# Sum t4 of the weight blocks moved from VectorE to an accumulating DMA, and gate chunk 3 put on seven block products

## The chip, the cores and the metric

The kernel runs on one core of a Trainium2 chip. The metric is the device time of one execution in microseconds; lower is better. The kernel before takes 1500.86 us, the median of three runs (1500.27 to 1501.66).

## The reference, cut to what matters

One decoder block on a 256 x 2048 input, all in float32. Nearly all the work is in products of a 256-row activation with weight matrices:

```python
h = rms_norm(x, norm_mix_pre)
p, q, k, v, g_lr, r, gate_logits = split_combined(h @ w_in)
y_a = pool_mixer(p, w_pool, pool_scale) @ w_branch_a
o = gla_chunked(q, k, v, log_sigmoid(g_lr @ w_gate_up + b_gate) / 16)
y_b = (rms_norm(o, gla_norm) * silu(r)) @ w_branch_b
gates = sigmoid(gate_logits + b_branch_gates)
mixed = (gates[0] * y_a + gates[1] * y_b) @ w_out
x = x + rms_norm(mixed, norm_mix_post)
h = rms_norm(x, norm_ffn_pre)
f = (silu(h @ w_ffn_gate) * (h @ w_ffn_up)) @ w_ffn_down
return x + rms_norm(f, norm_ffn_post)
```

## The kernel before, in words

**Chunks.** Every weight matrix is taken in chunks of 512 columns, and each chunk is one Job. plan() (L55) lists them in order: chunks of w_in (p, r, q, k), w_branch_a, w_in again (v, and eight "gates" chunks), w_branch_b (b), w_out (out), then for three parts of the feed-forward layer the pairs gate/up and four "down" chunks. The rows of weights run over tiles of 128 (kt is their number, 16 for most chunks, 12 for "down" in the third part). The last value that plan() yields says whether a chunk is "fast".

**Float32 in three products.** A weight w is split into wh, its rounding to the format that TensorE multiplies, and wl, the rest. ScalarE makes wh (an ACTIVATE with a copy) and VectorE makes wl (a subtraction). The activation is split in the same way, and each product is wh by high, wl by high, wh by low.

**Plain chunks.** A Step (L296) takes two weight tiles of 128 x 512: SP loads them into a "raw" buffer (L307, three buffers), L316 makes wh, L320 makes wl, and 12 matmuls of 512 columns follow (L347 to L349).

**Fast chunks.** The first eight weight tiles of a fast chunk are handled as a product of two-by-two blocks, by seven block products in place of eight. The blocks of weights are b11, b12 (the first block tile) and b21, b22 (the second). SP loads each block tile with two DMAs of 512 KB (L978) into one of three buffers. The products are Parts (L353), called q1, r5, q6, q7, q2, q4 and r3. Each has 12 matmuls of 256 columns (L407 to L409), wh from L383 and wl from L387. The weights of the Parts are:

- q1: b11 as loaded; q2: b21 as loaded; r3: b22 as loaded
- r5: b12 + b11, made in the place of b12 by an accumulating DMA that GpSimd issues (L379)
- q6: t2, the former plus b22, again in the place of b12 (L368, VectorE)
- q7: t2 - b11, in the place of b11 (L370, VectorE)
- q4: t4 = b21 + t2, in the place of b21 (L372, VectorE)

The remaining eight weight tiles (four in the third part of "down") are Steps, called m0 to m3 here.

**Order.** Job.merged (L281) sets the order of the units. q1, r5, q6 and q7 of a fast chunk stand between the last units of the chunk before. Where two fast chunks follow each other, the order of the units is q2, m0, q4, q1', r3, r5', m1, q6', m2, q7', m3, and then q2', m0', q4' and so on; a dash marks the following chunk, and this document calls such a place a join. prepare_to (L981) makes wh and wl up to four units ahead of TensorE (BUFS), makes the sums of a Part two units ahead, and starts the DMA for r5 up to seven units ahead (SUMS_AHEAD). blocks() (L967) loads the block tiles when a buffer comes free: the buffer of a first block tile is given on after q4, that of a second one after r3. A scheduler puts the instructions of each engine into their final order.

**Small work.** When a chunk ends, its done function takes the results out of PSUM; for "gates" (L763) that is L768, a sigmoid, and L772. Other small work stands in the queue bg and is taken one piece per unit: after gates chunk 1 these are the six pieces of combine (L221), which make the sums of the activation's blocks for the "b" chunks with L230, L241, L235 and L236.

Of the kernel before, what the change touches and what calls it, by code (L numbers as in the profile page):

```python
# [12 lines left out]
ALU = mybir.AluOpType  # L13
# [13 lines left out]
CW = 512  # L27
# [18 lines left out]
OFF_P, OFF_Q, OFF_K, OFF_V, OFF_G, OFF_R, OFF_GA = 0, 1024, 2048, 3072, 5120, 5136, 7184  # L46
# [8 lines left out]
def plan():  # L55

    kt = D // P
    for kind, off, n in [("p", OFF_P, 2), ("r", OFF_R, 4), ("q", OFF_Q, 2), ("k", OFF_K, 2)]:
        for i in range(n):
            low = kind == "r" and i == 0  # L60
            yield kind, i, "w_in", 0, kt, OFF_G if low else off + i * CW, CW + RANK if low else CW, False
    for n in range(4):
        yield "a", n, "w_branch_a", 0, kt // 2, n * CW, CW, False
    for n in range(4):
        yield "v", n, "w_in", 0, kt, OFF_V + n * CW, CW, False
    for n in range(8):
        yield "gates", n, "w_in", 0, kt, OFF_GA + n * CW, CW, n in (2, 4, 5, 6, 7)
    for n in range(4):
        yield "b", n, "w_branch_b", 0, kt, n * CW, CW, n in (1, 3)
    for n in range(4):  # L70
        yield "out", n, "w_out", 0, kt, n * CW, CW, n < 3
    chunks = DFF // CW
    for part in range(3):
        ms = range(part * 4, min(part * 4 + 4, chunks))
        for m in ms:
            yield "gate", m, "w_ffn_gate", 0, kt, m * CW, CW, m > 0
            yield "up", m, "w_ffn_up", 0, kt, m * CW, CW, m > 0
        for n in range(4):
            yield "down", (part, n), "w_ffn_down", part * 16, 4 * len(ms), n * CW, CW, (part, n) != (2, 3)


def packed(name, w):

    import numpy as np

    out = []
    for _, _, which, k0, kt, c0, width, fast in plan():
        if which != name:
            continue
        rows = w[0, k0 * P:(k0 + kt) * P, c0:c0 + width].reshape(kt, P, width)  # L90
        if fast:
            for b in range(2):
                blocks = rows[b * 4:b * 4 + 4].reshape(4, P, 2, HW)
                out.append(blocks.transpose(2, 1, 0, 3).ravel())
            rows = rows[4 * FAST:]
        out.append(rows.reshape(-1, GK, P, width).transpose(0, 2, 1, 3).ravel())
    return np.concatenate(out)
# [3 lines left out]
def tile_hybrid_block(ctx: ExitStack, tc: tile.TileContext, *aps):  # L101
# [4 lines left out]
    act, dve, pool, pe, sync = nc.scalar, nc.vector, nc.gpsimd, nc.tensor, nc.sync  # L106
# [14 lines left out]
    def nm(s):  # L121
        uid[0] += 1
        return f"{s}_{uid[0]}"
# [10 lines left out]
    def f32(ap):  # L134
        return ap.bitcast(F32)
# [68 lines left out]
    class Act:  # L204


        def __init__(self, name, groups, tag):
            self.name = name
            self.hi = [one.tile([P, 4, T], F32R, tag=f"{tag}{g}h", name=f"{name}{g}h") for g in range(groups)]
            self.lo = [one.tile([P, 4, T], F32R, tag=f"{tag}{g}l", name=f"{name}{g}l") for g in range(groups)]  # L210
# [48 lines left out]
    class Job:  # L259
# [4 lines left out]
        def __init__(self, w, at, kt, width, fast, lhs, done, across=False, head=0, tail=0):  # L264
            self.w, self.at, self.lhs, self.kt, self.width, self.done = w, at, lhs, kt, width, done
            self.across, self.groups, self.ps, self.extra, self.fast = across, kt // GK, None, None, fast
            both = tuple(range(NT))
            self.blocks = []
            self.early = [Part(self, n) for n in EARLY] if fast else []
            w = [Step(self, g) for g in range(FAST * 4 // GK if fast else 0, self.groups)]  # L270
            m = [(w[g], (t,)) for t in both for g in range(head)]
            m += [(x, both) for x in w[head:len(w) - tail]]
            m += [(x, (t,)) for t in both for x in w[len(w) - tail:]]
            self.units = m
            if fast:
                q2, q4, r3 = [(Part(self, n), both) for n in ("q2", "q4", "r3")]
                self.units = [q2, m[0], q4, r3] + m[1:] if len(m) > 2 else [q2, q4, r3] + m
            for w, ts in self.units:
                w.uses += 1
# [16 lines left out]
    class Step:  # L296
# [13 lines left out]
        def sum(self):  # L310
            pass
# [6 lines left out]
        def low(self):  # L318
            self.lo = wp.tile([P, GK, self.j.width], F32R, tag="wl", name=nm("wl"))
            dve.tensor_tensor(self.lo, self.raw, f32(self.hi), op=ALU.subtract)  # L320
# [32 lines left out]
    class Part:  # L353
# [8 lines left out]
        def sum(self):  # L362
            b11, b12 = self.block((0, 0)), self.block((0, 1))
            b21, b22 = (self.block((1, 0)), self.block((1, 1))) if len(self.j.blocks) > 1 else (None, None)
            if self.part == "r5":
                self.start_sum()
            elif self.part == "q6":
                dve.tensor_tensor(b12, b12, b22, op=ALU.add)  # L368
            elif self.part == "q7":
                dve.tensor_tensor(b11, b12, b11, op=ALU.subtract)  # L370
            elif self.part == "q4":
                dve.tensor_tensor(b21, b21, b12, op=ALU.add)  # L372
            self.src = {"q1": b11, "r5": b12, "q6": b12, "q7": b11, "q2": b21, "q4": b21, "r3": b22}[self.part]

        def start_sum(self):

            if not self.begun and self.j.blocks:
                self.begun = True
                pool.dma_start(self.block((0, 1)), self.block((0, 0)), accum_op=ALU.add)  # L379

        def high(self):
            self.hi = wp.tile([P, 4, HW], F32R, tag="wh", name=nm("wh"))
# [2 lines left out]
        def low(self):  # L385
            self.lo = wp.tile([P, 4, HW], F32R, tag="wl", name=nm("wl"))
            dve.tensor_tensor(self.lo, self.src, f32(self.hi), op=ALU.subtract)  # L387

        def left(self, i):
            lhs, p = self.j.lhs(), self.part  # L390
            if p in COMBOS:
                while p not in getattr(lhs, "x", {}):
                    (bg.popleft() if bg else soon.pop(0)[1])()
                return tuple(a[:, i] for a in lhs.x[p])
            return lhs.get(i if p == "q1" else 4 + i, 1 if p == "q4" else 0)
# [549 lines left out]
    for kind, n, name, k0, kt, c0, width, fast in plan():  # L945
        jobs.append(Job(source[name], at[name], kt, width, fast, **kinds[kind](n)))
        at[name] += kt * P * width
# [19 lines left out]
    def blocks():  # L967

        while held and held[0] < counts_["low"]:
            held.popleft()  # L970
        while pending and pending[0][0] <= counts_["low"] + AHEAD and len(held) < BLOCKS:
            _, until, j, rows_ = pending.popleft()
            tile_ = blk.tile([P, 2, 4, HW], F32, tag="blocks", name=nm("blocks"))
            j.blocks.append(tile_)
            n = 4 * P * HW
            for i in range(2):
                at = j.at + (rows_ * 2 + i) * n
                sync.dma_start(tile_[:, i], j.w[at:at + n].rearrange("(p k c) -> p k c", p=P, k=4))  # L978
            held.append(until)

    def prepare_to(n):  # L981
        while counts_["low"] < min(n, len(order)):
            at = counts_["low"]
            blocks()
            for w in order[at:at + SUMS_AHEAD]:
                if w.part == "r5":
                    w.start_sum()
            while counts_["sum"] < min(at + 2, len(order)):
                w = order[counts_["sum"]]
                w.sum()  # L990
                counts_["sum"] += 1
            order[at].high()
            order[at].low()
            counts_["low"] += 1
        blocks()

    for c in range(1, 4):
        prepare_to(c)
        load_x(c)
# [12 lines left out]
    for n, (j, w, ts) in enumerate(units):  # L1012
        prepare_to(released + BUFS)
        if n < 7:
            transpose_in(xa, hT, n + 1, "pre")
        due = [x for x in soon if x[0] <= 0]
        soon = [[n_ - 1, f] for n_, f in soon if n_ > 0]
        for _, f in due:
            f()
        w.multiply(ts)  # L1020
        left[w] -= 1
        while released < len(order) and not left[order[released]]:
            released += 1
        ended = tuple(t for t in ts if w.part not in EARLY and last[j if w.j is j else w.j, t] == n)
        if ended:
            w.j.done(w.j, ended)
        elif bg:
            bg.popleft()()
# [50 lines left out]
```

## Time and profile before

| | us |
|---|---|
| median of three runs (1500.27 to 1501.66) | 1500.86 |
| the profiled execution | 1499.66 |
| its span, first to last instruction | 1497.9 |
| its busy TensorE / VectorE / ScalarE / GpSimd | 1481.0 / 1185.1 / 887.3 / 64.8 |
| the 41 sums of t4 on VectorE (L372) | 50.2 |
| the 41 issues of the accumulating DMA on GpSimd (L379) | 35.4 |

PE is the matmul row of TensorE, DVE is VectorE, ACT is ScalarE, POOL is GpSimd, SPq and POOLq are the queues of SyncE and GpSimd that issue DMAs. In the rows of a timeline the first two numbers are the start and the busy time, in microseconds from the start of the span; what ended an idle time before an instruction is given in brackets. Matmuls overlap, so the time of a unit is read from start to start and not from the sum of its rows.

### The profile page before, as it was taken

The page shows a single profiled execution, that of the slowest core. Times are in us where ns is not written, and L with a number is a line of the kernel's source. Part 1 is how long each engine was busy: PE and PEld are TensorE (multiplying, and loading weights), DVE is VectorE, ACT ScalarE, POOL GpSimd, SP SyncE. Part 2 cuts the span into 40 slices and gives each one's busy share as a digit, 9 for nine tenths or more (in the row PEclk, how much of TensorE's full clock was granted, in tenths as well). Part 3 has the DMA queues.
Part 4 walks back from the last instruction along what each step waited for, and adds up shares of the span by engine and source line. Part 5 has one row for each costly group of instructions (what it writes and reads, how often), then busy time and mean ns, then how long its engine had stood idle before and what let it go on. Part 6 is the DMA issues. An engine that isn't in the chain of part 4 may idle for free.

```text
span 1497.9 us, 23015 instructions
## 1 busy us (share of the span) xinstructions
PE 1481.0 (99%) x8976; PEld 1306.7 (87%) x8976; DVE 1185.1 (79%) x1319; ACT 887.3 (59%) x1150; POOL 64.8 (4%) x91
## 2 busy tenths in 40 slices
PE   9999999999999999999999999999999999999997
PEld 8988999888888888889878989998989888988886
DVE  5755445885578897799768899887889898889996
ACT  6366433555455665556656666666666665666663
POOL 2000000000000000000000000000000000000001
PEclk9999999999999999999999999999999999999999
DMA  9746655345555688558855677767776776677654
GB/s 303 265 160 196 186 186 179 127 128 166 158 174 187 196 250 259 198 169 274 261 184 155 213 223 222 226 215 225 236 217 212 229 225 218 224 232 228 201 176 141
DMA packets 85869, 307.84 MB, mean 206 GB/s; under 512 B 9804, under 2 KB 10016, under 8 KB 85504
## 3 DMA queue, kind: packets, MB, share of 16 engines
q1 hardware_dynamic: 77616, 279.15, 55.6%
q0 software_dynamic: 7440, 25.97, 9.0%
q8 instruction: 70, 1.15, 0.3%
q10 hardware_dynamic: 704, 1.25, 0.3%
q14 instruction: 39, 0.32, 0.1%
HBM read 282.74 MB, written 2.10 MB: 190 GB/s over the span
## 4 chain that ended last, share of the span: by engine, by line
PE 90%; DVE 4%; issue 3%; DMA 2%; ACT 1%; POOL 0%; SPq 0%; DVEq 0%; POOLq 0%; ACTq 0%
PE acc L347 17%; PE acc L349 17%; PE acc L348 17%; PE ac L408 5%; PE ac L407 5%; PE ac L409 5%; PE acc L409 4%; PE acc L407 4%; PE acc L408 4%; PE acc L338 3%; PE acc L336 3%; PE acc L337 3%; PE tr L662 1%; DMA raw<-in_w_in_dram 1%; PE tr L179 1%
## 5 line engine op out<-in xcount | busy, mean ns | idle before, releaser
L316 ACT ACTIVATE wh<-raw 128x1024 fp32r<-128x1024 f32 (+1 forms) x356 | 376.7, 1059 | 360.3 <-PE acc L349 186.3
L320 DVE TENSOR_TENSOR wl<-raw,wh 128x1024 fp32r<-128x1024 f32 (+1 forms) x356 | 435.1, 1224 | 183.1 <-ACT wh L316 181.5
L387 DVE TENSOR_TENSOR wl<-blocks,wh 128x1024 fp32r<-128x1024 f32 x287 | 348.9, 1222 | 73.9 <-ACT wh L383 70.4
L383 ACT ACTIVATE wh<-blocks 128x1024 fp32r<-128x1024 f32 x287 | 301.7, 1058 | 143.3 <-PE acc L349 57.1
L409 PE MATMUL ac<-wh,x 128*128 128x256 f32 x336 | 94.1, 280 | 0.0
L408 PE MATMUL ac<-wl,x 128*128 128x256 f32 x336 | 94.1, 280 | 0.0
L407 PE MATMUL ac<-wh,x 128*128 128x256 f32 x336 | 94.0, 280 | 0.0
L379 POOL DMA_DIRECT2D blocks<-blocks x41 | 35.4, 864 | 811.8 <-DVE wl L320 329.7
L347 PE MATMUL acc<-wh,h22h 128*128 128x512 f32 x176 | 70.3, 399 | 0.2 <-ACT wh L316 0.2
L348 PE MATMUL acc<-wl,h22h 128*128 128x512 f32 x176 | 69.4, 394 | 0.0
L349 PE MATMUL acc<-wh,h23l 128*128 128x512 f32 x176 | 69.4, 394 | 0.0
L347 PE MATMUL acc<-wh,h23h 128*128 128x512 f32 x176 | 69.3, 395 | 0.1
L349 PE MATMUL acc<-wh,h22l 128*128 128x512 f32 x176 | 69.2, 394 | 0.0
L348 PE MATMUL acc<-wl,h23h 128*128 128x512 f32 x176 | 69.1, 393 | 0.0
L407 PEld LDWEIGHTS ac<-wh,x 128*128 128x128 f32 x336 | 63.1, 188 | 2.6
L408 PEld LDWEIGHTS ac<-wl,x 128*128 128x128 f32 x336 | 63.0, 188 | 2.5
L409 PEld LDWEIGHTS ac<-wh,x 128*128 128x128 f32 x336 | 63.6, 189 | 0.0
L372 DVE TENSOR_TENSOR blocks<-blocks,blocks 128x1024 f32<-128x1024 f32 x41 | 50.2, 1224 | 1.1
L368 DVE TENSOR_TENSOR blocks<-blocks,blocks 128x1024 f32<-128x1024 f32 x41 | 50.1, 1222 | 0.9
L347 PE MATMUL acc<-wh,h2h 128*128 128x512 f32 (+1 forms) x128 | 50.3, 393 | 0.0
L370 DVE TENSOR_TENSOR blocks<-blocks 128x1024 f32<-128x1024 f32 x41 | 50.0, 1219 | 0.1
L348 PE MATMUL acc<-wl,h3h 128*128 128x512 f32 (+1 forms) x128 | 49.8, 389 | 0.0
(540 smaller groups left out, 4126.1 us busy)
## 6 DMA issues: line engine op xcount, KB each, us to landing
raw<-in_w_in_dram SPq DMA_DIRECT2D x148, 512.0 KB, 3.6
raw<-in_w_ffn_gate_dram SPq DMA_DIRECT2D x48, 512.0 KB, 4.4
raw<-in_w_ffn_up_dram SPq DMA_DIRECT2D x48, 512.0 KB, 4.7
blocks<-in_w_ffn_down_dram SPq DMA_DIRECT2D x44, 512.0 KB, 4.3
raw<-in_w_ffn_down_dram SPq DMA_DIRECT2D x44, 512.0 KB, 4.4
blocks<-blocks POOLq DMA_DIRECT2D x41, 512.0 KB, 6.0
blocks<-in_w_ffn_gate_dram SPq DMA_DIRECT2D x40, 512.0 KB, 4.3
blocks<-in_w_ffn_up_dram SPq DMA_DIRECT2D x40, 512.0 KB, 4.4
```

Of the source, the lines that this page charges most:

```text
L316: act.activation(self.hi, self.raw, AF.Copy)
L320: dve.tensor_tensor(self.lo, self.raw, f32(self.hi), op=ALU.subtract)
L347: pe.matmul(ps, ah, hi[:, i, cs], start=first, stop=False, skip_group_check=j.fast)
L348: pe.matmul(ps, ah, lo[:, i, cs], start=False, stop=False, skip_group_check=j.fast)
L349: pe.matmul(ps, al, hi[:, i, cs], start=False, stop=last, skip_group_check=j.fast)
L368: dve.tensor_tensor(b12, b12, b22, op=ALU.add)
L372: dve.tensor_tensor(b21, b21, b12, op=ALU.add)
L383: act.activation(self.hi, self.src, AF.Copy)
L387: dve.tensor_tensor(self.lo, self.src, f32(self.hi), op=ALU.subtract)
L407: pe.matmul(dst, ah, wh, start=i == 0 and p in ("q1", "r5"), stop=False, skip_group_check=True)
L408: pe.matmul(dst, ah, wl, start=False, stop=False, skip_group_check=True)
L409: pe.matmul(dst, al, wh, start=False, stop=i == 3 and p in EARLY, skip_group_check=True)
```

## The change

Two things change. First, chunk 3 of the gates is fast too. Second, t4 is no longer a sum on VectorE in the place of b21. An accumulating DMA, issued by GpSimd, adds b21 onto t2, in the place of b12. It may start when t2 has been used twice: by the split for q6 (its wl is the last reader) and by the sum for q7; t2_used counts that. q4 then splits b12.

```diff
-        yield "gates", n, "w_in", 0, kt, OFF_GA + n * CW, CW, n in (2, 4, 5, 6, 7)
+        yield "gates", n, "w_in", 0, kt, OFF_GA + n * CW, CW, n > 1
...
-            self.blocks = []
+            self.blocks, self.t2_used = [], 0
...
             elif self.part == "q7":
                 dve.tensor_tensor(b11, b12, b11, op=ALU.subtract)
+                self.j.t2_used += 1
             elif self.part == "q4":
-                dve.tensor_tensor(b21, b21, b12, op=ALU.add)
-            self.src = {"q1": b11, "r5": b12, "q6": b12, "q7": b11, "q2": b21, "q4": b21, "r3": b22}[self.part]
+                self.start_sum()
+                assert self.begun
+            self.src = {"q1": b11, "r5": b12, "q6": b12, "q7": b11, "q2": b21, "q4": b12, "r3": b22}[self.part]
 
         def start_sum(self):
 
-            if not self.begun and self.j.blocks:
+            j = self.j
+            if not self.begun and (j.t2_used == 2 if self.part == "q4" else j.blocks):
                 self.begun = True
-                pool.dma_start(self.block((0, 1)), self.block((0, 0)), accum_op=ALU.add)
+                pool.dma_start(self.block((0, 1)), self.block((1, 0) if self.part == "q4" else (0, 0)), accum_op=ALU.add)
...
             dve.tensor_tensor(self.lo, self.src, f32(self.hi), op=ALU.subtract)
+            self.j.t2_used += self.part == "q6"
...
-                if w.part == "r5":
+                if w.part in ("r5", "q4"):
                     w.start_sum()
```

Lines L353 to L400 of the kernel before stand three lines lower in the changed one (L387 becomes L390, L379 becomes L382), later ones four (L768 becomes L772, L978 becomes L982).

**The queue of SP at a join of the feed-forward layer, before.** blocks_10058 is the second block tile of the following chunk, blocks_9887 and blocks_10097 are first block tiles, and the raw buffers are m0, m1, m2 and m3 of one chunk:

```order
L978 DMA blocks_9887<-in_w_ffn_gate_dram 128x1024 x2
L307 DMA raw_10032<-in_w_ffn_up_dram 128x1024
L307 DMA raw_10129<-in_w_ffn_up_dram 128x1024
L307 DMA raw_10169<-in_w_ffn_up_dram 128x1024
L978 DMA blocks_10058<-in_w_ffn_gate_dram 128x1024 x2
L307 DMA raw_10204<-in_w_ffn_up_dram 128x1024
L978 DMA blocks_10097<-in_w_ffn_up_dram 128x1024 x2
```

The same place in the changed kernel, where blocks_10118 is the second block tile of the following chunk:

```order
L982 DMA blocks_9947<-in_w_ffn_gate_dram 128x1024 x2
L307 DMA raw_10092<-in_w_ffn_up_dram 128x1024
L307 DMA raw_10189<-in_w_ffn_up_dram 128x1024
L307 DMA raw_10229<-in_w_ffn_up_dram 128x1024
L307 DMA raw_10265<-in_w_ffn_up_dram 128x1024
L982 DMA blocks_10118<-in_w_ffn_gate_dram 128x1024 x2
L982 DMA blocks_10157<-in_w_ffn_up_dram 128x1024 x2
```

The load of the second block tile has moved behind the raw buffer of m3. It goes into the buffer of an older first block tile, whose last reader was the sum L372 before and is the wl of q4 now.

**VectorE at the start of gates chunk 3, before** (a plain chunk there). The first two rows are the first piece of combine, L241, L236 and L230 are further pieces, and each L320 is the wl of a Step:

```order
L230 TENSOR_TENSOR scr_4382<-o0h,o0l 128x512
L230 TENSOR_TENSOR scr_4384<-o1h,o1l 128x512
L320 TENSOR_TENSOR wl_4390<-raw_4386,wh_4388 128x1024
L241 TENSOR_TENSOR scr_4384<-scr_4382,scr_4384 128x512
L320 TENSOR_TENSOR wl_4411<-raw_4407,wh_4409 128x1024
L236 TENSOR_TENSOR ox_4363<-scr_4384,ox_4362 128x512
L230 TENSOR_TENSOR scr_4425<-o0h,o0l 128x512
L320 TENSOR_TENSOR wl_4432<-raw_4428,wh_4430 128x1024
```

The same place in the changed kernel, now a join of gates chunks 2 and 3. The two L390 are the wl of r3 and of r5', L368 is the sum for q6', and the L320 is the wl of m1:

```order
L230 TENSOR_TENSOR scr_4383<-o0h,o0l 128x512
L230 TENSOR_TENSOR scr_4385<-o1h,o1l 128x512
L390 TENSOR_TENSOR wl_4389<-blocks_3902,wh_4387 128x1024
L241 TENSOR_TENSOR scr_4385<-scr_4383,scr_4385 128x512
L390 TENSOR_TENSOR wl_4411<-blocks_4091,wh_4409 128x1024
L236 TENSOR_TENSOR ox_4363<-scr_4385,ox_4363 128x512
L230 TENSOR_TENSOR scr_4425<-o0h,o0l 128x512
L368 TENSOR_TENSOR blocks_4091<-blocks_4091,blocks_4336 128x1024
L241 TENSOR_TENSOR scr_4383<-scr_4425,scr_4383 128x512
L320 TENSOR_TENSOR wl_4433<-raw_4429,wh_4431 128x1024
```

The sum for q6' has come in ahead of the wl of m1, among the pieces of combine. The rows that follow, as far as the wl of m2:

```order
L236 TENSOR_TENSOR ox_4366<-scr_4383,ox_4365 128x512
L241 TENSOR_TENSOR scr_4425<-scr_4385,scr_4425 128x512
L390 TENSOR_TENSOR wl_4457<-blocks_4091,wh_4455 128x1024
L236 TENSOR_TENSOR ox_4361<-scr_4425,ox_4361 128x512
L230 TENSOR_TENSOR scr_4473<-o1h,o1l 128x512
L370 TENSOR_TENSOR blocks_4091<-blocks_4091 128x1024
L320 TENSOR_TENSOR wl_4480<-raw_4476,wh_4478 128x1024
```

Here the wl of q6' and the sum for q7' (L370) stand ahead of the wl of m2, and four more pieces of combine.

## The prediction

> **What bounds the kernel now.** First the page: busy time by engine.
>
> ```profile
> span 1497.9 us, 23015 instructions
> PE 1481.0 (99%) x8976; PEld 1306.7 (87%) x8976; DVE 1185.1 (79%) x1319; ACT 887.3 (59%) x1150; POOL 64.8 (4%) x91
> ```
>
> TensorE is busy for all but 17 us of the span. A share hides stages, so the next view is busy time by stretch: from left PE, PEld, DVE, ACT, POOL, then clock, DMA share and GB/s. The stretches are the gates and b chunks, the feed-forward layer from its first fast chunk on, and its third part.
>
> ```profile
> 430.00:600.00 170.00, 170.00 (x941) 146.50 (x940) 143.21 (x154) 102.08 (x126) 8.89 (x13) 1.00 0.70 218
> 820.00:1405.00 585.00, 585.00 (x3696) 525.30 (x3695) 516.40 (x517) 377.86 (x469) 23.13 (x27) 1.00 0.71 221
> 1405.00:1470.00 65.00, 63.41 (x412) 56.73 (x411) 63.73 (x69) 43.24 (x61) 2.83 (x4) 1.00 0.59 186
> ```
>
> In the first two TensorE never waits, though VectorE is busy for 84% and 88%. Only in the third is VectorE as full as TensorE (63.73 and 63.41 of 65 us), and only there does TensorE wait for wh or wl. Its two longest waits from 1400 to 1475 us (in all, times, longest):
>
> ```profile
> PE acc L347 <- ACT wh L316: 0.6, 1, 0.6
> PE ac L407 <- ACT wh L383: 0.5, 1, 0.5
> ```
>
> So time taken off VectorE is worth something in the last 65 us, 1.6 us at most (65.00 - 63.41). Elsewhere the bound is the number of matmuls.
>
> **Chunk 3 in seven products: the matmuls.** What a unit takes is read from TensorE's timeline, start to start, at one join. The units are m3, q2', m0', q4', q1'', r3', r5'', m1':
>
> ```profile
> 1060.99 0.40 PE L347 MATMUL acc<-wh,h23h 128*128 128x512 f32 x1
> ...
> 1063.76 0.28 PE L407 MATMUL acc<-wh,h21h 128*128 128x256 f32 x1
> ...
> 1065.12 0.40 PE L347 MATMUL acc<-wh,h22h 128*128 128x512 f32 x1
> ...
> 1067.89 0.28 PE L407 MATMUL acc<-wh,h21h 128*128 128x256 f32 x1
> ...
> 1069.25 0.28 PE L407 MATMUL ac<-wh,h20h 128*128 128x256 f32 x1
> ...
> 1070.67 0.28 PE L407 MATMUL acc<-wh,x 128*128 128x256 f32 x1
> ...
> 1072.05 0.28 PE L407 MATMUL ac<-wh,x 128*128 128x256 f32 x1
> ...
> 1073.46 0.39 PE L347 MATMUL acc<-wh,h22h 128*128 128x512 f32 x1
> ```
>
> A Step takes 2.77 us. q2 and q4 take 1.36 each, r3 1.38, q1 1.42, r5 1.41; q6 and q7, which write the same place as q1, I take at 1.41. Seven Parts make 9.75 us in place of four Steps, 11.08. **Term: -1.3 us.**
>
> **Chunk 3: what VectorE has to do there.** The Steps needed four wl; the Parts need seven, two sums and two subtractions of results, and they come just where the pieces of combine run. The rows of VectorE at that place before:
>
> ```profile
> 477.14 0.69 DVE L230 TENSOR_TENSOR scr<-o0h,o0l 128x512 f32<-128x512 f32 x1
> 477.74 0.69 DVE L230 TENSOR_TENSOR scr<-o1h,o1l 128x512 f32<-128x512 f32 x1
> 478.34 1.22 DVE L320 TENSOR_TENSOR wl<-raw,wh 128x1024 fp32r<-128x1024 f32 x1
> 479.48 0.68 DVE L241 TENSOR_TENSOR scr<-scr,scr 128x512 f32<-128x512 f32 x1
> 480.08 1.22 DVE L320 TENSOR_TENSOR wl<-raw,wh 128x1024 fp32r<-128x1024 f32 x1
> ```
>
> Back to back, a large operation advances VectorE by 1.14 us and a piece by 0.60. Up to 478.34 the work ahead is the same in both kernels, but for one t4 sum that ran earlier and had idle time behind it. TensorE stood here:
>
> ```profile
> 477.42 0.28 PE L407 MATMUL acc<-wh,h1h 128*128 128x256 f32 x1
> ...
> 478.83 0.28 PE L407 MATMUL acc<-wh,x 128*128 128x256 f32 x1
> ```
>
> q4 ended at 478.83. In the changed kernel q1', r3 and r5' follow (1.42 + 1.38 + 1.41), and m1 begins at 483.04. VectorE, from 478.34 by the changed order: wl of r3 (1.14), L241 (0.60), wl of r5' (1.14), L236 and L230 (1.20), the sum for q6' (1.14), L241 (0.60), so the wl of m1 starts at 484.16 and is there at 485.38, 2.1 us after its first use (483.27). Then two pieces, the wl of q6', two pieces and the sum for q7': the wl of m2 starts at 484.16 + 1.14 + 1.20 + 1.14 + 1.20 + 1.14 = 489.98 and is there at 491.20. Without waits m2 would need it at 483.04 + 2.77 + 1.41 + 0.23 = 487.45. TensorE is then 3.7 us late in all; it can take a few products with wh ahead, some 0.3 us. After that the lag ends: two pieces and two large operations lie between this and the wl of m3, 3.5 us for 4.2 us of TensorE. **Term: +3.4 us**, between 0 (if the pieces give way) and 5 (if ScalarE's roundings in between hold VectorE up).
>
> **t4 leaves VectorE.** The group of the sums on the page:
>
> ```profile
> L372 DVE TENSOR_TENSOR blocks<-blocks,blocks 128x1024 f32<-128x1024 f32 x41 | 50.2, 1224 | 1.1
> ```
>
> 50.2 us go, 1.22 a chunk. Since TensorE waited nowhere between 820 and 1405, this is worth 0 there.
>
> **t4 as a DMA: is it in time?** The trace has its like, the accumulating DMA for r5. Its rows are: issue over the whole run, time to landing from 820 to 1405, the share of the GpSimd queue in that stretch.
>
> ```profile
> L379 POOL DMA_DIRECT2D blocks<-blocks x41: 848/852/941, 31.9 to 1436.5; - x41
> ```
>
> ```profile
> DMA to landing us min/median/max: 5.0/6.0/8.0
> ```
>
> ```profile
> q0 software_dynamic: 3888, 14.16, 13.3%
> ```
>
> 27 issues (POOL, x27 above) in 13.3% of 585 us make 2.9 us of all 16 engines for one. The place is the join above. VectorE's rows are the wl of q6, the sum for t4, the wl of q4, the next sum for q6, and the wl of m1; then ScalarE's wh for q4, GpSimd's issue for r5, and SP's loads of the next second and first block tile:
>
> ```profile
> 1053.01 1.22 DVE L387 TENSOR_TENSOR wl<-blocks,wh 128x1024 fp32r<-128x1024 f32 x1
> ...
> 1059.64 1.23 DVE L372 TENSOR_TENSOR blocks<-blocks,blocks 128x1024 f32<-128x1024 f32 x1
> ...
> 1062.83 1.23 DVE L387 TENSOR_TENSOR wl<-blocks,wh 128x1024 fp32r<-128x1024 f32 x1 [0.38 <-ACT wh L383]
> ...
> 1070.44 1.23 DVE L368 TENSOR_TENSOR blocks<-blocks,blocks 128x1024 f32<-128x1024 f32 x1
> 1071.58 1.22 DVE L320 TENSOR_TENSOR wl<-raw,wh 128x1024 fp32r<-128x1024 f32 x1
> ```
>
> ```profile
> 1061.73 1.06 ACT L383 ACTIVATE wh<-blocks 128x1024 fp32r<-128x1024 f32 x1
> ```
>
> ```profile
> 1052.60 0.86 POOL L379 DMA_DIRECT2D blocks<-blocks  x1 [20.29 <-DVE wl L320]
> ```
>
> ```profile
> 1060.90 0.93 SPq L978 DMA_DIRECT2D blocks<-in_w_ffn_gate_dram  x2
> ...
> 1068.02 0.81 SPq L978 DMA_DIRECT2D blocks<-in_w_ffn_up_dram  x2
> ```
>
> t4 may start when the wl of q6 is done, at 1054.23. Alone it lands 6.0 us later, 1060.3; behind the DMA for r5 (1052.60 + 6.0 + 2.9) at 1061.5. ScalarE takes q4 at 1061.73. It is just in time by the medians and up to 1.8 us late by the longest landing (8.0). By itself that costs nothing: q4 starts on TensorE at 1067.89 and its wl is done at 1064.06. On GpSimd the next r5, due 20 us later, queues behind the wait.
>
> The Trainium skill (DMA: Bandwidth & Descriptors, "Anatomy of one DMA — SWDGE (gpsimd) path") fits such a DMA as 2.0 us plus bytes over 436 GB/s. For 512 KB that is an estimate of 3.2 us, and t4 would land at 1057.4 with 4 us to spare. The trace has 5.0 at least and does not agree; I go by the trace.
>
> **The load behind it.** The next second block tile goes into the buffer that q4 now reads last. Its load could start at 1060.90, after the sum; now it waits for the wl of q4, 1064.06. Behind it on SP stand the next first block tile, which waited until 1068.02 anyway, and the raw buffer of m0'; m3 has been moved ahead. How long these loads take, 820 to 1400:
>
> ```profile
> DMA to landing us min/median/max: 3.3/4.3/6.2
> ```
>
> The second of the pair follows 0.4 us behind the first, so the tile is there at 1068.8, by the longest at 1070.7; its sum starts at 1070.44. Behind the sum the wl of m1 ends at 1072.80, and TensorE wants it at 1073.46 + 0.23. Spare: 1.6 + 0.9 = 2.5 us. A late t4 (up to 1.8) or a slow load (up to 1.9) fits; both together miss by 1.2. The change has 38 such joins (5 in the gates, b to out and 2 in out, 30 in the feed-forward layer). **Term: 0**, bounds 0 and +1.2 a join.
>
> **The third part of "down".** Its chunks have two Steps, and r5' and r3 alone stand between the wl of q4 and the sum for q6'. VectorE's rows, the three wl and the sum:
>
> ```profile
> 1427.62 3.49 DVE L387 TENSOR_TENSOR wl<-blocks,wh 128x1024 fp32r<-128x1024 f32 x3
> 1431.20 1.23 DVE L368 TENSOR_TENSOR blocks<-blocks,blocks 128x1024 f32<-128x1024 f32 x1
> ```
>
> The wl of q4 is done at 1428.84; plus 0.4 + 4.3 the tile lands at 1433.5, 2.3 us after 1431.20. The sum of t4 ahead of it goes (1.2), so 1.1 us is lost, at two joins; against it stand the 1.6 us that TensorE already waits here for VectorE. **Term: +0.4**, between -1.6 and +2.5.
>
> **Sum.** -1.3 + 3.4 + 0 + 0.4 = +2.5 us. The profiled execution has 1499.66 (its span of 1497.9 and 1.8 around it) and would become 1502.2. It lies 1.2 below the median; on the median of 1500.86 the forecast is 1503.4. About 0.2%, 3.0 us, is what a measurement of this kernel can tell from no change.
>
> **The rivals.**
>
> 1. *Late joins, slower.* The 16 DMA engines get 2.9 us more per chunk of 20.8 us (4 x 2.77 + 9.75), so the share of 0.71 goes to 0.85, and landings move from median to longest. From the point where t4 and the load are late by more than 2.5 us together, every join costs. At 0.2 us for each of 38 it is +7.6, 1511.0. For it: both budgets are nearly used up. Against it: four units of wh and wl stand ready. Chance 0.17. One rule would take from the spare: by the Trainium skill (SBUF — State Buffer, "SBUF: two separate sides") VectorE in a two-port mode locks GpSimd out of a shared port for a whole instruction, so that it cannot write the DMA's descriptors. That would be up to 1.22 us here and would double this chance. The trace does not show it: 41 issues took 848 to 941 ns beside a VectorE that is busy for 88%.
> 2. *The lag at chunk 3 is absorbed.* The pieces of combine wait for ScalarE in between and the wl pass them, or TensorE's products with wh suffice. Then -1.3 + 0.4: 1500.0. Against it: an engine's order is fixed, and the pieces stand ahead of the wl. Chance 0.20.
> 3. *Faster.* No lag, and the waits of the last 65 us go with the sums: -1.3 - 1.6, 1498.0. For it: there VectorE is the bound. Against it: the loads there become late. Chance 0.13.
>
> The forecast, 1501.4 to 1505.4 by the bounds of its terms, has 0.50. Its upper part lies above 1503.9, so 0.30 of it is "same" and 0.20 "slower". Rival 1 adds 0.16 slower and 0.01 same, rival 2 0.19 same and 0.01 faster, rival 3 0.07 same and 0.06 faster: faster 0.07, same 0.57, slower 0.36. The range, 1498.6 to 1509.0, leaves out most of rival 3 and the upper half of rival 1.
>
> **What would show it.** TensorE should be busy without a gap from 820 to 1405; wait some 3 us near 483 to 491 for the wl of m1 and m2 (L320); the DMA for t4 should land 6 to 8 us after the wl of q6; ScalarE should wait for it by under 2 us; the second block tile's load should start 3 us later than before. Waits for L368 or its like on TensorE in the feed-forward layer would make the prediction wrong, and so would a TensorE that does not wait at 483.

## The result

The changed kernel takes 1544.53 us (median of four runs, 1543.89 to 1548.65) against 1501.11 for the kernel before: 1.0294 times as long, 95% interval 1.0282 to 1.0306. That is 43.4 us slower, where +2.5 was forecast with 1509.0 as the upper end. The profiled execution has 1543.89.

### The profile page after: what moved, and what is told of

Read it like the earlier page. It is cut to its first block, busy times and chain, and to the rows that moved or that the text cites. A ratio compares the mean times of both kernels' runs of the same rounds, so it can differ in the third digit from the quotient of the medians.

```text
span 1542.1 us, 23211 instructions
## 1 busy us (share of the span) xinstructions
PE 1493.8 (97%) x9012; PEld 1310.6 (85%) x9012; DVE 1138.4 (74%) x1285; ACT 890.3 (58%) x1157; POOL 102.0 (7%) x134
## 5 line engine op out<-in xcount | busy, mean ns | idle before, releaser
L320 DVE TENSOR_TENSOR wl<-raw,wh 128x1024 fp32r<-128x1024 f32 (+1 forms) x352 | 430.0, 1224 | 217.7 <-ACT wh L316 214.7
L316 ACT ACTIVATE wh<-raw 128x1024 fp32r<-128x1024 f32 (+1 forms) x352 | 372.0, 1058 | 338.8 <-PE acc L349 166.0
L390 DVE TENSOR_TENSOR wl<-blocks,wh 128x1024 fp32r<-128x1024 f32 x294 | 355.4, 1221 | 130.8 <-ACT wh L386 123.7
L386 ACT ACTIVATE wh<-blocks 128x1024 fp32r<-128x1024 f32 x294 | 306.4, 1057 | 188.2 <-DMA blocks<-blocks 70.5
L382 POOL DMA_DIRECT2D blocks<-blocks x84 | 72.5, 882 | 846.1 <-DVE blocks L370 258.9
L411 PE MATMUL ac<-wh,x 128*128 128x256 f32 x348 | 97.6, 280 | 2.6 <-ACT wh L386 2.6
L412 PE MATMUL ac<-wl,x 128*128 128x256 f32 x348 | 97.5, 280 | 0.0
L413 PE MATMUL ac<-wh,x 128*128 128x256 f32 x348 | 97.4, 280 | 0.0
L348 PE MATMUL acc<-wl,h22h 128*128 128x512 f32 x176 | 70.5, 400 | 0.6 <-DVE wl L320 0.5
L411 PEld LDWEIGHTS ac<-wh,x 128*128 128x128 f32 x348 | 65.4, 188 | 5.9 <-ACT wh L386 3.4
L413 PEld LDWEIGHTS ac<-wh,x 128*128 128x128 f32 x348 | 65.8, 189 | 0.1
L368 DVE TENSOR_TENSOR blocks<-blocks,blocks 128x1024 f32<-128x1024 f32 x42 | 51.3, 1221 | 5.0 <-DMA blocks<-in_w_ffn_down_dram 2.3
L370 DVE TENSOR_TENSOR blocks<-blocks 128x1024 f32<-128x1024 f32 x42 | 51.2, 1220 | 0.2
L348 PE MATMUL acc<-wl,h2h 128*128 128x512 f32 (+1 forms) x128 | 50.2, 392 | 0.9 <-DVE wl L320 0.9
```

The lines of the kernel that those rows point to most:

```text
L316: act.activation(self.hi, self.raw, AF.Copy)
L348: pe.matmul(ps, ah, lo[:, i, cs], start=False, stop=False, skip_group_check=j.fast)
L382: pool.dma_start(self.block((0, 1)), self.block((1, 0) if self.part == "q4" else (0, 0)), accum_op=ALU.add)
L386: act.activation(self.hi, self.src, AF.Copy)
L411: pe.matmul(dst, ah, wh, start=i == 0 and p in ("q1", "r5"), stop=False, skip_group_check=True)
L412: pe.matmul(dst, ah, wl, start=False, stop=False, skip_group_check=True)
```

## The profile after

The page of the changed kernel, with the lines that answer to those of before:

```profile
span 1542.1 us, 23211 instructions
PE 1493.8 (97%) x9012; PEld 1310.6 (85%) x9012; DVE 1138.4 (74%) x1285; ACT 890.3 (58%) x1157; POOL 102.0 (7%) x134
q0 software_dynamic: 13632, 48.51, 17.5%
DMA 15%; PE 12%; issue 7%; DVE 6%; ACT 3%; POOL 1%; SPq 0%; POOLq 0%; ACTq 0%; DVEq 0%
L386 ACT ACTIVATE wh<-blocks 128x1024 fp32r<-128x1024 f32 x294 | 306.4, 1057 | 188.2 <-DMA blocks<-blocks 70.5
blocks<-blocks POOLq DMA_DIRECT2D x84, 512.0 KB, 7.2
```

The fourth line's counterpart before:

```profile
PE 90%; DVE 4%; issue 3%; DMA 2%; ACT 1%; POOL 0%; SPq 0%; DVEq 0%; POOLq 0%; ACTq 0%
```

VectorE has lost 46.7 us of work (1185.1 to 1138.4), as meant, and TensorE still counts as busy for 97%. The fourth line is the one to read: the chain of work that ended last. Before, it was TensorE's work for 90% of the span. In the changed kernel the profile can follow the chain back only to 861 us, so its shares add up to 44%, and of these DMA has 15 and TensorE 12. ScalarE stood idle 70.5 us for DMAs from blocks to blocks, and these are now 84 and take 7.2 us to land (median).

Busy time by stretch, in the columns that the prediction gave; the stretches are those whose matmuls are the same as in the three of before:

```profile
430.30:611.20 180.90, 172.59 (x977) 147.54 (x976) 141.38 (x155) 104.36 (x131) 14.76 (x20) 1.00 0.73 218
839.30:1443.00 603.70, 590.88 (x3694) 526.72 (x3693) 481.32 (x490) 377.32 (x468) 46.35 (x54) 1.00 0.82 238
1443.00:1514.20 71.20, 65.62 (x414) 58.68 (x413) 60.08 (x65) 44.19 (x61) 5.47 (x7) 0.98 0.65 189
```

170 us became 180.9, 585 became 603.7, 65 became 71.2. TensorE was busy without a gap in the second stretch before; now it idles 12.8 us there, and counts as busy 5.9 us longer for the same products. The clock is 1.00 there as before.

One join of the feed-forward layer in the timeline. GpSimd's rows are r5 and then t4, ScalarE's is the wh of q4, VectorE's are its wl and the products that end an "up" chunk (L881). TensorE's are the last matmul of that chunk and the transposition of what L881 makes:

```profile
1101.43 0.85 POOL L382 DMA_DIRECT2D blocks<-blocks  x1 [19.16 <-DVE blocks L370]
1102.44 0.85 POOL L382 DMA_DIRECT2D blocks<-blocks  x1 [0.16 <-issue]
...
1110.63 0.40 PE L349 MATMUL acc<-wh,h23l 128*128 128x512 f32 x1
...
1111.62 2.95 ACT L386 ACTIVATE wh<-blocks 128x1024 fp32r<-128x1024 f32 x3 [2.66 <-DMA blocks<-blocks]
1112.71 1.23 DVE L390 TENSOR_TENSOR wl<-blocks,wh 128x1024 fp32r<-128x1024 f32 x1 [3.16 <-ACT wh L386]
1113.85 1.28 DVE L881 TENSOR_TENSOR scr<-acc,scr 128x512 f32<-128x512 f32 x2
1113.96 0.80 SPq L982 DMA_DIRECT2D blocks<-in_w_ffn_up_dram  x2
...
1114.68 0.30 PE L179 MATMUL tr<-ident,scr 128*128 128x128 f32 x1 [2.29 <-ACT wh L386]
```

The line of the DMAs, taken for these two issues alone, gives their landings, r5's first:

```profile
DMA to landing us min/median/max: 5.9/5.9/5.9
DMA to landing us min/median/max: 9.1/9.1/9.1
```

Two things go wrong behind the 9.1 us. VectorE stands 3.16 us before the wl of q4, and L881 stands behind that in its queue, though the chunk that it reads was done on TensorE at 1111.03. TensorE has then only q2 of the next chunk to do, and waits 2.29 us until L881 has run. (The row names an L386, the third of its group, which ended within 0.1 us of the first L881.) Over the whole second stretch, TensorE's two largest waits are these (in all, times, longest):

```profile
PE tr L179 <- DVE scr L881: 6.7, 15, 1.2
PE tr L179 <- ACT wh L386: 5.2, 3, 2.3
```

They make 11.9 of the 12.8 us that it idles there. Measured from start to start, the steps to and between the transpositions behind the ten "up" chunks have grown by 15.3 us, of the 18.7 that the stretch has grown.

The second thing: SP's load of the next second block tile starts only at 1113.96, when the wl of q4 has freed the buffer. The Trainium skill (TensorE: Matmul & The Clock Gate, "Architectural detail: the array is 16× 32×32, not 1× 128×128") has ScalarE's and VectorE's queues as strictly first in, first out; the trace agrees: L881, whose input was there at 1111.03, starts at 1113.85, behind the late wl.

Some of the longest pieces of the chain, and one issue on GpSimd (start, us, what):

```profile
927.71 7.73 DMA blocks<-blocks
937.76 1.29 DVE scr L881 x2
...
1038.80 8.98 DMA blocks<-blocks
1053.83 4.39 DMA blocks<-in_w_ffn_up_dram
1058.98 0.85 POOL blocks L382
1059.88 9.15 DMA blocks<-blocks
...
1075.07 4.61 DMA blocks<-in_w_ffn_gate_dram
1081.42 8.82 DMA blocks<-blocks
```

Both show. Near 930 the chain leaves the DMA for t4 through L881. From 1038 to 1081 it runs from t4 to a block load and on to the next t4, with no matmul in it: a ring, 21.1 and 21.5 us round. The sum of the units of a chunk is 20.8, and in the kernel before the issues for r5 at this place follow each other in 21.1 to 21.2 us, so a round of the ring costs little by itself. The load in it (1053.83) is that of a first block tile. Its buffer is freed by the wl of r3, which stands behind the wl of q4; r5's DMA waits for it (issue at 1058.98), and t4's is issued right behind r5's. The other way round, by the second block tile, the sum for q6 and its wl, is 0.3 us shorter there: this wl ends at 1059.52.

## The experiments

Beside each time stands where it was lost. The same matmul, counted from the program's end (for 450 us, ahead of chunk 3, from its start), is looked up in the trace of the run and of before; the table has the growth of the difference between 450, 530, 800, 1425 and 1480 us of before (us; the columns are the first joins with chunk 3, the rest of the gates to out, the feed-forward layer up to its third "down", and that):

| kernel | time (its before) | 450-530 | 530-800 | 800-1425 | 1425-1480 |
|---|---|---|---|---|---|
| changed | 1544.5 (1501.1) | 5.0 | 14.1 | 18.5 | 6.4 |
| e1 chunk 3 alone | 1504.5 (1500.5) | 2.4 | 1.9 | 0.4 | -0.1 |
| e2 t4 alone | 1547.6 (1500.5) | 0.0 | 10.6 | 30.8 | 4.9 |
| e3 t4 on VectorE | 1506.2 (1500.5) | 2.4 | 2.0 | 0.4 | 0.4 |
| e4 t4 ahead of r5 | 1513.9 (1500.5) | 4.5 | 1.5 | 2.0 | 6.3 |
| e5 block tiles | 1524.2 (1500.3) | 3.6 | 1.5 | 13.5 | 6.1 |
| e6 e4, third part on VectorE | 1508.3 (1500.3) | 3.0 | 2.4 | 3.2 | 0.0 |
| e7 half of t4 | 1522.3 (1500.3) | 4.0 | 5.9 | 9.3 | 5.0 |
| e8 e5 without chunk 3 | 1517.4 (1500.3) | 0.0 | 3.2 | 13.7 | 4.1 |
| e9 e5, t4 ahead | 1509.6 (1501.0) | 2.4 | 0.4 | 1.8 | 3.9 |
| e10 e5, q4 later | 1511.2 (1501.0) | 2.3 | 2.1 | 0.0 | 5.1 |
| e11 all cures, no chunk 3 | 1500.9 (1501.0) | 0.0 | -0.3 | 1.4 | -0.7 |
| e12 q4 later | 1523.5 (1500.4) | 4.6 | 7.5 | 2.1 | 9.4 |

Each trace is one execution. Those of e7 and e8 lie 3.5 and 4.2 us above the median of their kernel, so their columns add up to more than the difference of the medians.

### The two edits apart: e1, e2

```diff
 # e1, from before                       # e2, from the changed kernel
-... n in (2, 4, 5, 6, 7)               -... n > 1
+... n > 1                              +... n in (2, 4, 5, 6, 7)
```

> The kernel before with only the gate chunk 3 by seven block products; t4 stays on VectorE. Theory A (nearly all of the loss is a closed chain around the DMA for t4; chunk 3 is the prediction's own term): +2 to +4 us over before, 1503 to 1505, since in the changed kernel TensorE is 3.7 us behind the kernel before at 500 us (4.05 less the 0.32 that it was behind at 450). The prediction's terms for chunk 3 give +2.1. If the lag at chunk 3 is itself the DMA's doing: 1499.8, -1.3.

> The changed kernel with gate chunk 3 back as four Steps; t4 is an accumulating DMA. Theory A: the whole loss but chunk 3's share, 1539 to 1542. If the loss needs both edits together: near 1501 to 1510.

e1 takes 1.0024 times before (1.0015 to 1.0033), +4.0 us, and e2 1.031 (1.029 to 1.033), 47.1 us and more than the whole change, where 1539 to 1542 was expected. So t4 alone makes the large loss. Chunk 3 is a small term, as the prediction said; TensorE's waits from 470 to 530 us in e1 (in all, times, longest):

```profile
PE ac L407 <- ACT wh L383: 2.7, 2, 1.5
PE acc L348 <- DVE wl L320: 0.2, 1, 0.2
```

### Release or transfer: e3

```diff
-                self.start_sum()
-                assert self.begun
+                dve.tensor_tensor(b12, b12, b21, op=ALU.add)
...
-                if w.part in ("r5", "q4"):
+                if w.part == "r5":
```

> The changed kernel, but t4 is summed by VectorE (b12 + b21, into the place of t2), so that the first block tile is still released only by the wl of q4, and there is one accumulating DMA a chunk as before. Theory A (the chain wl of q4, load of the second block tile, sum for q6, its wl, DMA for t4, wh and wl of q4 takes 21 to 23 us where TensorE needs 20.85; the DMA is 7 to 9 us of it with its wait): with 1.2 us in its place the chain is near 14 us and nothing is lost by it; 1502 to 1506, chunk 3's share alone. Rival B (the second accumulating DMA slows every transfer): also 1502 to 1506. Rival C (the late release of the buffer is enough by itself): near 1540.

1.0038 (1.0024 to 1.0051), 1506.2 us, and by stretch the same as e1. Rival C falls: the place of t2 and the later release cost nothing while VectorE does the sum. Between theory A and rival B this run does not choose, since both gave the same time.

### The order of two issues: e4

```diff
-                pool.dma_start(...)
+                d = pool.dma_start(...)
+                if self.part == "r5":
+                    tc.keep_in_program_order(d)
```

> The changed kernel with one order kept on GpSimd: the DMA for r5 of the next chunk is issued behind the DMA for t4 and not ahead of it. Bytes, buffers and VectorE's work are the same. Theory A: t4 lands 4 to 6 us after its issue and not 6 to 8, the chain is 18 to 20 us, under 20.85, and the loss is mostly gone: 1503 to 1510. Rival B (traffic): as slow as the changed kernel, 1540 to 1545. Rival C (late release): the same 1540 to 1545.

The scheduler may move an instruction ahead of others; the added line keeps r5's DMA behind t4's. 1.0089 (1.0075 to 1.0102): two issues on GpSimd changed places, and 30 of the 43 us are gone. At 1513.9 it is still above the 1503 to 1510 that was expected. ScalarE's wait for these DMAs over the whole run, 70.5 us 34 times before the swap:

```profile
ACT wh L388 <- DMA blocks<-blocks: 7.8, 5, 3.8
```

The bytes are the same, so rival B, the traffic, is not the cause of these 30. GpSimd's two issues in a join, now t4 and then r5:

```profile
1061.68 1.76 POOL L382 DMA_DIRECT2D blocks<-blocks  x2 [19.20 <-DVE wl L392]
```

The line of the DMAs for the first of them alone:

```profile
DMA to landing us min/median/max: 7.0/7.0/7.0
```

t4 lands 7.0 us after its issue and not 9.1. Read issue by issue from 839 to 1425 us of each trace, the median for t4 is 6.0 us here and 8.3 in the changed kernel; 4 to 6 was expected. What the swap takes away is mainly this landing behind r5's. The issue of r5 held t4's up by 0.4 us at most in the join of 1101.43, where t4's last input, the wl of q6, was done at 1102.08.

### Half the bytes: e7

```diff
+                dve.tensor_tensor(b12[:, :2], b12[:, :2], b21[:, :2], op=ALU.add)
                 self.start_sum()
...
+                k = slice(2 if self.part == "q4" else 0, 4)
-                pool.dma_start(self.block(...), self.block(...), accum_op=ALU.add)
+                pool.dma_start(self.block(...)[:, k], self.block(...)[:, k], accum_op=ALU.add)
```

> The changed kernel with t4's DMA behind r5's, but half as large: k tiles 0 and 1 are summed by VectorE. Theory A: the DMA lands some 5.5 to 6 us after its issue (7.7 less half of the 3.5 that a whole one takes in the queue), about what it takes ahead of r5, so the chain is as long as there: 1510 to 1518. If what counts is the order of the issues, or that one more DMA is issued at all, and not the time to landing: 1535 to 1545.

1.0145 (1.0129 to 1.0162), 1522.3 us, slower than expected. The issues of e7:

```profile
blocks<-blocks POOLq DMA_DIRECT2D x42, 512.0 KB, 6.2
blocks<-blocks POOLq DMA_DIRECT2D x42, 256.0 KB, 7.0
```

Half as many bytes take t4's landing from 8.3 us to 7.0 (medians), not to the 5.5 to 6 that were expected: most of the time does not go with the bytes. With r5's issue still ahead of it, e7's t4 comes later than e4's and earlier than the changed kernel's, and its loss lies between theirs; the sign was right, the size was not.

### The buffer: e5, e8

```diff
-BLOCKS = 3
+BLOCKS = 6
...
-            tile_ = blk.tile([P, 2, 4, HW], F32, tag="blocks", name=nm("blocks"))
-            j.blocks.append(tile_)
+            tile_ = blk.tile([P, 4, HW], F32, tag="blocks", name=nm("blocks"))
+            j.blocks[which] = tile_
...
+            pending.append((by["q1"], by["q7"], j, (0, 0)))
+            pending.append((by["q1"], by["q4"], j, (0, 1)))
+            pending.append((by["q6"], by["r3"], j, (1, 1)))
+            pending.append((by["q6"], by["q4"], j, (1, 0)))
```

> The changed kernel, t4's DMA still behind r5's, but each 4 KB block has a tile of its own (six instead of three pairs, the same memory), and b22 is loaded ahead of b21, so that b22 goes into the place of the earlier b11, free since the wl of q7, and the sum for q6 no longer waits for the wl of q4. DMA traffic is the same, and t4 should still land 7 us after its issue. Theory A (closed chain through the buffer): the loss of the feed-forward layer (18.5 us from 800 to 1425) and of the gates to out (11) is gone, of chunk 3 stays: 1503 to 1510. Rival B (t4 is late by itself, or the transfers crowd each other): 1530 to 1545.

> A tile for each block, t4 as a DMA, and the gate chunks of the kernel before (chunk 3 in four Steps). Theory A: no closed chain and no chunk 3 term: 1498 to 1504, the 50.2 us taken from VectorE being worth 1.6 at most. Rival B: 1527 to 1542.

1.0149 (1.0134 to 1.0164) and 1.011 (1.0088 to 1.0131), 1524.2 and 1517.4 us: both miss both of the ranges that were expected. Theory A, the ring through the buffer, was half right. From the gates to out the 14.1 us have become 1.5; in the feed-forward layer 13.5 of 18.5 are still there. The rest of the cause is in e5's timeline and in its waits of TensorE after 500 us:

```profile
1138.04 2.95 ACT L386 ACTIVATE wh<-blocks 128x1024 fp32r<-128x1024 f32 x3 [2.44 <-DMA blocks<-blocks]
1139.13 1.23 DVE L390 TENSOR_TENSOR wl<-blocks,wh 128x1024 fp32r<-128x1024 f32 x1 [2.95 <-ACT wh L386]
1140.27 1.28 DVE L881 TENSOR_TENSOR scr<-acc,scr 128x512 f32<-128x512 f32 x2
1141.01 0.33 PE L179 MATMUL tr<-ident,scr 128*128 128x128 f32 x1 [1.98 <-DVE scr L881]
```

```profile
PE tr L179 <- DVE scr L881: 8.8, 18, 2.0
```

The buffer is free in time, but t4 itself is not there, and L881 stands behind q4. That became theory A2.

### The place in the queue: e9, e10, e12

```diff
 # e9: e5 with e4's edit.  e10: e5, e12: the changed kernel, each with
-                return u[:3] + [e[0], u[3], e[1], u[4], ...
+                return u[:2] + [e[0], u[3], u[2], e[1], u[4], ...
```

> A tile for each block and t4's DMA ahead of r5's. Theory A2 (two losses: the closed chain through the buffer, and t4 landing late in its own join, where wh of q4 stands in ScalarE's queue and wl of q4 in VectorE's with the products of the up chunk (L881) behind it, for which TensorE waits): both are cut, so the feed-forward layer before its third part loses nothing, that part still loses 6 (t4 is late there by itself): 1508 to 1512. If tiles of blocks themselves cost something (their loads come singly): 1515 to 1524, as slow as with r5 first (1524.2).

> A tile for each block, r5's DMA first, and q4 two units later in a join (q2, m0, q1, r3, q4, r5 for q2, m0, q4, q1, r3, r5), so that t4 has 2.8 us more and the wl of q4 no longer stands ahead of L881. The third part of down keeps its order. Theory A2: what the tiles of blocks left from 800 to 1425 (13.5 us) is mostly gone, the third part's 6 stays: 1509 to 1514. If the loss that is left is the crowding of transfers and not the place of q4 in the queues: 1520 to 1525.

> The changed kernel (tiles of pairs, r5's DMA first) with only q4 two units later in a join. In the feed-forward layer up to its third part the changed kernel lost 18.5 us, 13.5 with tiles of blocks, 0 with those and q4 later. If the late q4 in front of L881 is the main loss there and the buffer a small one: 0 to 5 lost there; from the gates to out, where the buffer's chain is the main loss (15, and 1.3 with tiles of blocks), the wl of q4 now stands behind that of r3 and the loss stays or grows: 1523 to 1535 in all. If the closed chain through the buffer is a loss of its own in the feed-forward layer too: 10 or more there, 1535 to 1545.

1.0059 (1.0043 to 1.0074), 1.0063 (1.0049 to 1.0077) and 1.0153 (1.0135 to 1.0172), each in the first of its two expected ranges, e12 at the lower end. e10 keeps r5 in front and all the traffic, and loses nothing from 800 to 1425. e12 keeps the pairs of blocks too, and loses 2.1 there; in that stretch TensorE no longer waits for L881 at all, and its waits are these two:

```profile
PE ac L412 <- DVE wl L390: 0.2, 1, 0.2
PE acc L348 <- DVE wl L320: 0.2, 1, 0.2
```

So in the feed-forward layer the late wl of q4 ahead of L881 is the main cause and the ring a small one. The edit does two things for it at once: it gives t4 2.8 us more, and it takes the wl of q4 from in front of L881. t4 in time is enough by itself: e4 leaves the place as it was and loses 2.0 in that stretch. The place alone, with t4 as late as in the changed kernel, no run has; but in eight joins of e12 ScalarE still waits for t4, 6.9 us in all, and TensorE loses next to nothing by it. From the gates to out e12 still loses 7.5 and e5 1.5: there it is mostly the ring. That e12 halves the loss there was not expected, and neither was its third part, where it loses 9.4 in place of 6.4 (e9 and e10 lose 3.9 and 5.1 there, where 6 was expected). The parts do not add up; that each cure also takes time from the other chain is likely, but not shown.

### The third part of "down": e6, and everything: e11

```diff
+                if self.j.kt < 16:
+                    dve.tensor_tensor(b12, b12, b21, op=ALU.add)
+                else: ...
```

> The kernel with t4 ahead of r5 (1513.9), and in the third part of down t4 back on VectorE, in the place of t2. Theory A: in that part a chunk is two Steps shorter, 15.3 us, and the chain of some 19 us costs the difference at two joins, 6.2 us in the two runs with t4 as a DMA; with VectorE summing it is short: 1506 to 1509. If the third part loses to VectorE's own work or to the last loads: no change from 1513.9.

> A tile for each block, t4's DMA ahead of r5's, in the third part of down t4 on VectorE in the place of t2, and the gate chunks of the kernel before. Theory A2: every loss is cut and VectorE has 45 us less to do, which TensorE did not wait for: 1499 to 1503, no gain over before (1500.3). If time taken off VectorE is worth something by itself: 1490 to 1497.

e6: 1.0047 (1.0032 to 1.0062), the 6.3 us of that part are gone. e4's timeline shows the longest of the waits that made them up, with the wl of q4 late as above:

```profile
1435.53 2.95 ACT L388 ACTIVATE wh<-blocks 128x1024 fp32r<-128x1024 f32 x3 [2.50 <-DMA blocks<-blocks]
1436.63 1.23 DVE L392 TENSOR_TENSOR wl<-blocks,wh 128x1024 fp32r<-128x1024 f32 x1 [3.03 <-ACT wh L388]
1438.60 0.30 PE L179 MATMUL tr<-ident,scr 128*128 128x128 f32 x1 [2.06 <-ACT wh L388]
```

e11: 1.0002 (0.9993 to 1.001). Its page:

```profile
span 1498.9 us, 23142 instructions
PE 1481.1 (99%) x8976; PEld 1306.9 (87%) x8976; DVE 1140.0 (76%) x1281; ACT 888.0 (59%) x1150; POOL 98.8 (7%) x129
```

VectorE has 45 us less to do than before, TensorE the same 99%, and the time is that of before, within 1.5 us by the interval. No version that was run is faster than the kernel before.

## Why the prediction was wrong

- **Chunk 3, -1.3 + 3.4 = +2.1: right in size, but not in the wait that it named.** e1 lost 2.4 us there in its trace; its median, +4.0 (2.3 to 5.0 by the interval), holds 1.9 more at the next chunks, of which one wait of 1.07 us for ya was not foreseen. VectorE's order and times were as worked out. TensorE's two long waits, 2.7 us, were for the wh of Parts behind the sums, and not for the wl of m1 and m2.
- **t4 leaves VectorE, worth 0: right** within 1.5 us (e11).
- **"By itself that costs nothing: q4 starts on TensorE at 1067.89 and its wl is done at 1064.06": the step that failed.** The landing was sized about 1 us too short (8.9 us after r5's issue was forecast; 10.1 in the join of 1101.43), and ScalarE's wait "by under 2 us" was 2.66 there. The larger mistake is that I asked only when TensorE needs q4. What waits is what stands behind the wl of q4 in VectorE's queue, and that is L881, which TensorE needs at once: 15.3 of the 18.7 us in the feed-forward layer stand there, and 2.1 are left when q4 comes later (e12). I named that rule for GpSimd's queue and did not apply it to the two where the late operand is read.
- **"Spare: 2.5 us ... both together miss by 1.2. Term: 0": failed too.** It treats each join as if it began on time. A late t4 makes the wl of q4 and of r3 late, these the two block loads, and the loads the next t4, by r5's issue ahead of it or by the sum for q6. Once this ring is closed, a spare in it is used up. From the gates to out, opening it takes 12.6 of 14.1 us away (e5). In the feed-forward layer it costs little: three rounds, from 1038.80 to 1102.44, set the changed kernel back by 0.7 us, and the one transposition of 1114.68 by 2.8. The bound that I wrote down, +1.2 at each of 38 joins, is +45.6. That the loss of +43.4 is near it is luck, since the loss does not come at 1.2 a join and most of that in the feed-forward layer is not the ring's. But the bound was mine, and the forecast of 1501.4 to 1505.4 "by the bounds of its terms" left it out; even rival 1 took only 0.2 a join.
- **Order on GpSimd.** I put r5's DMA ahead of t4's, rightly, and made it a matter of 1.2 us in t4's landing. The order is worth 30 us of the time (e4).
- **The third part, +0.4: mis-sized**, 6.4. Its sum counted the load behind q4 but not the wait for t4 itself. With VectorE doing the sum in that part, nothing is lost there (e6).
- **Rival 1** had the direction with 0.17, and its ground ("both budgets are nearly used up") was right for the ring, though not for L881. The objection "four units of wh and wl stand ready" fails because L881 is not one of them. The locked port that would have doubled its chance is not seen in the changed kernel either: the 84 issues take 848 to 1194 ns, median 855.

What stays open is how the loss of the gates to out divides among its joins, and why e2 loses more in the feed-forward layer (30.8) than the changed kernel (18.5) with the same code there. Of these 12.3 us, 9.0 fall between 1300 and 1425 us of before. There e2's block tiles land in 4.4 to 5.5 us and those of the changed kernel in 3.9 to 4.0 (medians); what makes its loads slower, no run shows. The difference also shows how far a column of one trace can be trusted.

## What to carry to other kernels

When work moves from an engine to a DMA, the price is not the engine's time saved but the latency on the path from the last input to the first reader: list what stands behind that reader in its queue, and follow the buffer that it frees until the path either ends or comes round; a ring has to be shorter than the period, because a spare in it is used up once. If two DMAs of one queue come due together, issue the one with the earlier reader first. A bound worked out per join has to enter the range times the number of joins.

## What the runs showed of the hardware

The queues from 839.30 to 1443.00 in the changed kernel (packets, MB, share of 16 engines):

```profile
q1 hardware_dynamic: 31388, 114.30, 53.3%
q0 software_dynamic: 7920, 28.84, 27.9%
```

A packet of the accumulating DMAs, which go from SBUF to SBUF, holds an engine for 0.34 us (0.279 x 16 x 603.7 / 7920), one of the loads from HBM for 0.16 (0.533 x 16 x 603.7 / 31388). One packet in nine has 4 bytes alone; for the 4 KB packets the means are 0.38 and 0.18. So the accumulating DMA takes twice the time on the engines for the same bytes. Whether the adding or the other path does that, no run separates. Yet the time to landing follows the bytes only in part: t4 lands in 8.3 us with 512 KB and in 7.0 with 256 KB (e7), both behind r5's. Two in a row do not take twice as long: issued 1.0 us apart they land after 5.9 and 9.1 us, so both are there 10.1 us after the first issue, and not 11.8. The Trainium skill (DMA: Bandwidth & Descriptors, "Two DMAs through the same engine are not ordered") says that descriptors of one queue of a DMA engine start in order but are pipelined, and the trace agrees with the second.
